# A sixth place for raw weights, spread additions of the seven products, and transposes in a second matrix bank, in a two-layer hybrid decoder on one core

## The chip, the core and the metric

The kernel runs on one core of one Trainium2 chip. Its metric is the device time of one execution in microseconds (us). A core has a matrix engine (TensorE, PE in the profile; its weight loads are shown as PEld), a vector engine (VectorE, DVE), a scalar engine (ScalarE, ACT), GpSimd (POOL) and a queue engine (SyncE, SP) that here issues the loads of weights. Operands lie in an on-chip memory of 128 partitions; products of TensorE are summed in eight banks of a separate memory.

## The reference

256 tokens of width 2048 pass through two layers: differential attention and then a Mamba-2 mixer, each followed by a dense MLP with a squared ReLU, all in float32.

```
for i in range(2):
    hn = rms_norm(h, mixer_norm[i])
    h = h + (diff_attention if i == 0 else mamba2_mixer)(hn, ...)
    h = h + sq_relu_mlp(rms_norm(h, mlp_norm[i]), mlp_w1[i], mlp_w2[i])

sq_relu_mlp(h, w1, w2) = jnp.square(jax.nn.relu(h @ w1)) @ w2    # w1: 2048 x 8192, w2: 8192 x 2048
```

Only the two MLPs matter here. The change also deepens the buffer through which all weights of the kernel pass.

## The kernel before

**How products are kept exact.** Each float32 weight tile of 128x1024 is split into a high part (a cast on ScalarE, L158) and a rest (a subtraction on VectorE, L159); activations are split in the same way (L263, L264, L273, L274). Each product is then three matmuls: high by high, high by rest, rest by high.

**The places.** A raw weight tile is loaded by SyncE into one of five places with the tag `raw` (L183 to L186). Its split goes to one of four places with the tag `w`. The load of a tile waits until the last reader of the earlier tile in its place is done, and SyncE issues its loads strictly one after another. Of the eight banks of TensorE's output memory, three have the tag `aux`, one `aux1`, and four `mm` (the function `bank`, tiles named `pp`).

**The MLP.** The hidden width 8192 is cut into eight blocks of 1024 columns. The first block ("s" in `MLP_KINDS`) is computed plainly by `blocks`: its result is hidden features by tokens, and its activations are split by `expand` straight from `u`. The other seven ("S") are computed by `seven`, a Strassen-like scheme: for each of four slices of the inner width it loads four quarters of the weights, forms sums of them on VectorE (L569, L579, L584, L600, one tile of 128x1024 each), splits them and makes seven products p1 to p7 of a half size, each in a bank of its own. After p1 and p5 come p7, p3 and p6, and last p2 and p4. The sums of products that make the four quarters of the result are formed in `u` on VectorE (L587 to L591, L603, L604), then squared after a ReLU on ScalarE. The result is tokens by features, so `expand` transposes it on TensorE: eight groups of four 128x128 transposes for two blocks (L656), each group in an `aux` bank, from which ScalarE and VectorE split it (L263, L264).

`sum_parts` makes the sums of the activations for the seven products: eight rounds, each with a tile `a` and a tile `asum` from the MLP's own pool (tag `relu`, one place for each).

**The order of the work.** `mlp` first runs blocks 0 and 1 interleaved (`both(0, 28/12)`), with the rounds of `sum_parts` as side work. Then for q = 0 to 3 it multiplies the pair of blocks 2q, 2q+1 by w2 (`token_steps`, L238 and L240, eight steps for each of four column blocks j) while the steps of the next pair's `seven` are interleaved at a fixed rate (`work`, `rate`). `expand` of the pair is put into the side queue at the start of each q. The order in which the instructions stand on each engine is then set by a scheduler in the toolchain, which weighs when places and operands come free; the code's order is only where it starts. So a change of places can move instructions far from the lines that were edited.

In the profile, the first MLP runs from about 404 to 1092 us and the second from about 1765 to 2447 us. The stretch of `both(0)` is 404 to 490 us in the first MLP; the pairs of blocks change over at about 490, 658 and 827 us, and in the second MLP 1358 us later.

Of the kernel before, what the change touches and what calls it, by code (L numbers as in the profile page):

```python
# [20 lines left out]
P = 128  # L21
# [70 lines left out]
def trunk_kernel(ctx: ExitStack, tc: tile.TileContext, x, xt, par, rope, qk, wv, wo, w10, w10s, w20, win, wdt, wout, w11, w11s, w21, out):  # L92
# [25 lines left out]
    def aux():  # L118
        return ps.tile([P, 512], F32, tag="aux", bufs=3, name="aux")
# [60 lines left out]

    def load(src, n=1):

        raw = wp.tile([P, 1024], F32, tag="raw", bufs=5, name="raw")  # L183
        w = 1024 // n
        for i in range(n):
            nc.sync.dma_start(out=raw[:, i * w:(i + 1) * w], in_=src[:, i * w:(i + 1) * w])  # L186
        return raw
# [137 lines left out]
    with tc.tile_pool(name="xin", bufs=1) as xp:  # L325
        raw, xf = [], []
        for s in range(2):
            pool = (wp, xp)[s]
            raw.append([pool.tile([P, 1024], F32, tag="raw", bufs=(5, 4)[s], name="raw") for _ in range(4)])
        for g in range(4):  # L330
            for j in range(2):
                xf.append(xp.tile([P, 2, T], F32, tag="xf", bufs=8, name="xf"))
                nc.sync.dma_start(out=xf[-1], in_=x[2 * g + j])
                if j == 0:
                    for b in range(4):
                        c = slice(512 * (g % 2), 512 * (g % 2 + 1))
                        nc.sync.dma_start(out=raw[g // 2][b][:, c], in_=qk[b, g // 2][:, c])
        w = None
        for g in range(4):
            if g % 2 == 0:  # L340
                w = [wp.tile([P, 2, 1024], F32R, tag="w", bufs=4, name="w") for _ in range(4)]
            for j in range(2):
                xs += x_parts(xf[2 * g + j], 2 * g + j, C_MIX0)
            for b in range(4):
                c = slice(512 * (g % 2), 512 * (g % 2 + 1))
                src = raw[g // 2][b][:, c]
                S.copy(out=w[b][:, 0, c], in_=src)
                V.tensor_tensor(out=w[b][:, 1, c], in0=src, in1=w[b][:, 0, c].bitcast(F32), op=ALU.subtract)
                for i in range(2):
                    for k in range(4):  # L350
                        kk = slice(512 * (g % 2) + k * P, 512 * (g % 2) + (k + 1) * P)
                        act = xs[4 * g + k]
                        if i == 0:
# [171 lines left out]

    def sum_parts(pool, x, dst):

        a = pool.tile([P, 2, T], F32, tag="relu", bufs=2, name="a")
        for i in range(2):
            V.tensor_tensor(out=a[:, i, :], in0=x[i][:, 0, :].bitcast(F32), in1=x[i][:, 1, :].bitcast(F32), op=ALU.add)  # L530
# [12 lines left out]
        s1, s2, s3, s4 = ([sa[:, i, n, :] for i in range(2)] for n in range(4))  # L543
        dst.append([[x0[:, i, 0:P] for i in range(2)], s4, [x1[:, i, 0:P] for i in range(2)], s1, s3, s2, [x1[:, i, P:T] for i in range(2)]])
        yield

    def seven(pool, src, sas, u):
# [42 lines left out]
        V.tensor_tensor(out=u[:, 0, 1], in0=p3, in1=u[:, 0, 1], op=ALU.add)  # L590
        V.tensor_tensor(out=u[:, 1, 1], in0=u[:, 1, 0], in1=u[:, 1, 1], op=ALU.subtract)  # L591
# [12 lines left out]
        V.tensor_tensor(out=u[:, 1, 0], in0=u[:, 1, 0], in1=p4, op=ALU.subtract)  # L604
        for t in range(2):
            S.activation(u[:, t, 0], u[:, t, 0], AF.Relu)
            S.activation(u[:, t, 0], u[:, t, 0], AF.Square)
        yield

    def mlp(xs, w1, w1s, w2, pool, after):  # L610
# [29 lines left out]
        def expand(c, hid, place=None):  # L640
# [8 lines left out]
            for j in range(0, 4, 2):  # L649
                axs = []  # L650
                for i in range(2):
                    ax = aux().rearrange("p (a b) -> p a b", a=2)
                    for f in range(2):
                        for t in range(2):
                            c = T * (j + i) + P * f
                            PE.transpose(ax[:, f, t * P:(t + 1) * P], uf[:, t, c:c + P], ident)  # L656
# [5 lines left out]
        def both(q, share):  # L662

            if not share:
                yield from hidden(2 * q)
# [18 lines left out]
        for _ in both(0, 28 / 12 if kinds[:2] == "sS" else 1.0):  # L684
            pass
        norm_mean()
        V.reciprocal(out=r2, in_=ms)
        for q in range(4):
            if q < 3:
# [387 lines left out]
```

## Time and profile before

| what | us |
|---|---|
| median of three runs (lowest, highest) | 2450.47 (2450.01, 2451.3) |
| profiled execution, its own time | 2449.62 |
| span of the profiled execution | 2447.9 |
| TensorE busy, by the page | 2434.1 |
| VectorE busy | 2098.2 |
| ScalarE busy | 1535.6 |
| share of 16 DMA engines of the queue that loads weights | 61.3% |

The span runs from the first to the last instruction; 1.7 us of the execution's time lie around it. The busy time of TensorE is that of overlapping records: a 128x512 matmul is recorded with 0.39 us, while the next one starts 0.227 us after it, so its modelled end hides the first 0.17 us of a wait. To find lost time on TensorE, the starts of neighbouring rows are to be compared.

### The profile page before, as it was taken

Reading aid. Unit: us, or ns where it says so; the run is one execution under the profiler, and the core shown is the slowest. Engines: PE = TensorE matmul, PEld = TensorE weight load, DVE = VectorE, ACT = ScalarE, POOL = GpSimd, SP = SyncE. Lnnn points to the kernel's source line nnn. Section 1 sums busy time; section 2 is a strip of 40 time slices with the busy share of each in tenths; the row PEclk is TensorE's granted clock in tenths of the full one; section 3 lists DMA queues with packets and bytes.
Section 4 is the critical chain, followed back from the end, with each engine's and each line's share of the span. In section 5 each row is a group of like instructions: output and inputs, shape, how many; then the busy total and the mean of one; then the engine's idle time right before and its main releaser. Section 6 shows DMA issues by size and latency. Waiting matters only on the chain.

```text
span 2447.9 us, 32626 instructions
## 1 busy us (share of the span) xinstructions
PE 2434.1 (99%) x12050; PEld 2038.8 (83%) x12050; DVE 2098.2 (86%) x2591; ACT 1535.6 (63%) x2154; POOL 1.2 (0%) x8
## 2 busy tenths in 40 slices
PE   9999999999999999999999999999999999999999
PEld 8888888878888788888888888888887888878887
DVE  6988879999998999568886887887899999899964
ACT  7666656666666666456776575775666666666653
POOL 0000000000000000000000000000000000000000
PEclk9999999999999999999999999999999999999999
DMA  8545555667667676556565556556566766776764
GB/s 287 164 157 175 167 175 194 208 232 243 230 208 230 221 231 218 191 177 211 190 198 196 174 198 199 166 189 191 190 218 220 239 229 203 238 232 206 233 205 147
DMA packets 140192, 500.54 MB, mean 204 GB/s; under 512 B 15648, under 2 KB 15840, under 8 KB 140032
## 3 DMA queue, kind: packets, MB, share of 16 engines
q1 hardware_dynamic: 137312, 489.75, 61.3%
q10 hardware_dynamic: 2720, 8.71, 1.0%
q8 instruction: 94, 1.54, 0.2%
q14 instruction: 66, 0.54, 0.1%
HBM read 496.24 MB, written 2.16 MB: 204 GB/s over the span
## 4 chain that ended last, share of the span: by engine, by line
PE 70%; DVE 18%; DMA 7%; issue 4%; ACT 1%; DVEq 0%; SPq 0%; ACTq 0%
PE pp L238 21%; PE pp L169 16%; DVE w L159 11%; PE pp L240 10%; PE pp L173 9%; PE aux L557 6%; DMA raw<-in_w11s 3%; DMA raw<-in_w10s 3%; PE aux L559 3%; DVE wsum L569 1%; DVE wsum L600 1%; DVE raw L579 1%; PE aux L878 1%; DVE h L716 1%; ACT w L158 1%
## 5 line engine op out<-in xcount | busy, mean ns | idle before, releaser
L159 DVE TENSOR_TENSOR w<-raw,w 128x1024 fp32r<-128x1024 f32 x858 | 1034.6, 1219 | 196.1 <-ACT w L158 193.5
L158 ACT CAST w<-raw 128x1024 fp32r<-128x1024 f32 x858 | 892.7, 1052 | 493.4 <-PE pp L238 316.3
L238 PE MATMUL pp<-w,act 128*128 128x512 f32 x3072 | 983.1, 391 | 0.7 <-ACT w L158 0.7
L238 PEld LDWEIGHTS pp<-w,act 128*128 128x128 f32 x3072 | 575.4, 188 | 121.7 <-ACT w L158 1.5
L240 PE MATMUL pp<-w,act 128*128 128x512 f32 x1536 | 598.5, 390 | 0.0
L169 PE MATMUL pp<-act,w 128*128 128x512 f32 x2000 | 489.0, 392 | 0.0
L169 PEld LDWEIGHTS pp<-act,w 128*128 128x128 f32 x2000 | 366.4, 188 | 72.6 <-issue 1.0
L240 PEld LDWEIGHTS pp<-w,act 128*128 128x128 f32 x1536 | 288.3, 188 | 58.0
L557 PE MATMUL aux<-w,sa 128*128 128x512 f32 x896 | 300.3, 392 | 5.2 <-DVE act L264 1.7
L173 PEld LDWEIGHTS pp<-act,w 128*128 128x128 f32 x2000 | 258.3, 191 | 11.0 <-issue 0.9
L173 PE MATMUL pp<-act,w 128*128 128x256 f32 x2000 | 266.8, 284 | 0.0
L158 ACT CAST w<-wsum 128x1024 fp32r<-128x1024 f32 x168 | 176.9, 1053 | 114.6 <-PE pp L238 43.8
L557 PE MATMUL aux<-w,act 128*128 128x512 f32 x672 | 228.8, 394 | 0.8 <-ACT w L158 0.3
L159 DVE TENSOR_TENSOR w<-wsum,w 128x1024 fp32r<-128x1024 f32 x168 | 204.8, 1219 | 1.9 <-ACT w L158 1.5
L557 PEld LDWEIGHTS aux<-w,sa 128*128 128x128 f32 x896 | 167.4, 188 | 44.3 <-DVE w L159 4.7
L559 PE MATMUL aux<-w,sa 128*128 128x512 f32 x448 | 175.2, 391 | 0.0
L557 PEld LDWEIGHTS aux<-w,act 128*128 128x128 f32 x672 | 124.8, 188 | 32.2 <-DVE w L159 6.2
L559 PE MATMUL aux<-w,act 128*128 128x512 f32 x336 | 131.4, 391 | 0.0
L559 PEld LDWEIGHTS aux<-w,sa 128*128 128x128 f32 x448 | 84.2, 188 | 16.7
L569 DVE TENSOR_TENSOR wsum<-raw 128x1024 f32<-128x1024 f32 x56 | 68.4, 1222 | 21.4 <-DMA raw<-in_w10s 11.5
L579 DVE TENSOR_TENSOR raw<-raw 128x1024 f32<-128x1024 f32 x56 | 68.5, 1222 | 20.4 <-DMA raw<-in_w11s 11.4
L600 DVE TENSOR_TENSOR wsum<-wsum,raw 128x1024 f32<-128x1024 f32 x56 | 68.0, 1220 | 7.4 <-DMA raw<-in_w11s 3.9
(218 smaller groups left out, 1736.0 us busy)
## 6 DMA issues: line engine op xcount, KB each, us to landing
raw<-in_w SPq DMA_DIRECT2D x288, 512.0 KB, 4.4
raw<-in_win SPq DMA_DIRECT2D x160, 512.0 KB, 4.1
raw<-in_w10s SPq DMA_DIRECT2D x140, 512.0 KB, 4.3
raw<-in_w11s SPq DMA_DIRECT2D x140, 512.0 KB, 4.3
raw<-in_wout SPq DMA_DIRECT2D x64, 512.0 KB, 4.1
raw<-in_qk SPq DMA_DIRECT2D x56, 512.0 KB, 4.3
raw<-in_wv SPq DMA_DIRECT2D x32, 512.0 KB, 4.2
raw<-in_wo SPq DMA_DIRECT2D x32, 512.0 KB, 4.2
```

The lines of the kernel that those rows point to most:

```text
L158: S.copy(out=wh[:, s], in_=raw[:, s])
L159: V.tensor_tensor(out=wl[:, s], in0=raw[:, s], in1=wh[:, s].bitcast(F32), op=ALU.subtract)
L169: PE.matmul(acc, lhsT=wk, rhs=acts[k0 + k], start=(start and k == 0), stop=False)
L173: PE.matmul(acc[:, 0, :], lhsT=wk, rhs=acts[k0 + k][:, 0, :], start=False, stop=(stop and k == 7))
L238: PE.matmul(pp[t], lhsT=act[:, 0, tok], rhs=m, start=(s + i + k == 0), stop=(s == n - 1 and i + k == 2))
L240: PE.matmul(pp[t], lhsT=act[:, 1, tok], rhs=m, start=False, stop=False)
L557: PE.matmul(pp, lhsT=ah, rhs=m, start=(i + kp + j == 0), stop=(i == 3 and kp + j == 2))
L559: PE.matmul(pp, lhsT=al, rhs=m, start=False, stop=False)
L569: V.tensor_tensor(out=a[i], in0=b11, in1=b12, op=ALU.subtract)
L579: V.tensor_tensor(out=b12, in0=b22, in1=b12, op=ALU.subtract)
L600: V.tensor_tensor(out=a[i], in0=a[i], in1=b21, op=ALU.subtract)
L716: V.scalar_tensor_tensor(out=h[:, t, cols(j)], in0=pp[t], scalar=r2[:, t:t + 1], in1=h[:, t, cols(j)], op0=ALU.mult, op1=ALU.add)
```

## The change

1. `raw` has six places and not five. The tiles `a` and `asum` of `sum_parts` are now taken from these six places (each uses half of one), and the tag `relu` is gone.
2. In `seven`, the additions that follow p6 and p7 stay where they were (L587, L588); the three others and their ReLU and square are done one at a time after slices 0, 1 and 2 of p2 and p4 (`u4`, `c12`, `c22`), and the addition of p2 comes with slice 3, ahead of that of p4.
3. The `expand` of block 0 is put into the side queue inside `both`, after the last step of block 0.
4. `expand` puts its second group of each pair of groups in a bank of `mm` (except for blocks 6 and 7, where `place` is set).

```
@@ load, and the first loads of attention
-        raw = wp.tile([P, 1024], F32, tag="raw", bufs=5, name="raw")
+        raw = wp.tile([P, 1024], F32, tag="raw", bufs=6, name="raw")
@@ sum_parts
-        a = pool.tile([P, 2, T], F32, tag="relu", bufs=2, name="a")
+        a = wp.tile([P, 1024], F32, tag="raw", bufs=6, name="a")[:, 0:2 * T].rearrange("p (a b) -> p a b", a=2)
...
-        f = pool.tile([P, 4, P], F32, tag="relu", bufs=2, name="asum")
+        f = wp.tile([P, 1024], F32, tag="raw", bufs=6, name="asum")[:, 0:4 * P].rearrange("p (a b) -> p a b", a=4)
@@ seven
-        V.tensor_tensor(out=u[:, 0, 1], in0=u[:, 0, 1], in1=u[:, 1, 1], op=ALU.subtract)
-        V.tensor_tensor(out=u[:, 0, 1], in0=p3, in1=u[:, 0, 1], op=ALU.add)
-        V.tensor_tensor(out=u[:, 1, 1], in0=u[:, 1, 0], in1=u[:, 1, 1], op=ALU.subtract)
-        for t in range(2):
-            S.activation(u[:, t, 1], u[:, t, 1], AF.Relu)
-            S.activation(u[:, t, 1], u[:, t, 1], AF.Square)
+        def u4():
+            V.tensor_tensor(out=u[:, 0, 1], in0=u[:, 0, 1], in1=u[:, 1, 1], op=ALU.subtract)
+        def c12():
+            V.tensor_tensor(out=u[:, 0, 1], in0=p3, in1=u[:, 0, 1], op=ALU.add)
+            relu2(0, 1)
+        def c22():
+            V.tensor_tensor(out=u[:, 1, 1], in0=u[:, 1, 0], in1=u[:, 1, 1], op=ALU.subtract)
+            relu2(1, 1)
+        late = [u4, c12, c22]
...
             product(p4, A22, split_weights(a[i]), i)
-            yield
-        V.tensor_tensor(out=u[:, 0, 0], in0=p2, in1=u[:, 0, 0], op=ALU.add)
+            if i < 3:
+                late[i]()
+            else:
+                V.tensor_tensor(out=u[:, 0, 0], in0=p2, in1=u[:, 0, 0], op=ALU.add)
+                relu2(0, 0)
+            yield
@@ expand
-                    ax = aux().rearrange("p (a b) -> p a b", a=2)
+                    ax = aux().rearrange("p (a b) -> p a b", a=2) if i == 0 or place is not None else bank()
@@ both
+            side.add(early)
             yield from b
```

How the scheduler's order moves, at three places of the first MLP (the numbers in names count tiles; a lower number was asked for earlier).

VectorE, in `both(0)`. `wsum_3958` is the first weight sum of the seven products and needs the loads `raw_3954` and `raw_3956`; `a_` and `asum_` are tiles of `sum_parts`. Before:

```order
L537 TENSOR_TENSOR asum_3913<-a_3910,asum_3913 128x128
L159 TENSOR_TENSOR w_3852<-raw_3850,w_3852 128x1024
L541 TENSOR_TENSOR sa_3936<-asum_3913,sa_3936 128x512
L319 TENSOR_TENSOR h_101<-pp_3652,h_101 128x512
L319 TENSOR_TENSOR h_101<-pp_3653,h_101 128x512
L159 TENSOR_TENSOR w_3884<-raw_3882,w_3884 128x1024
L530 TENSOR_TENSOR a_3947<-act_3699 128x256 x2
L569 TENSOR_TENSOR wsum_3958<-raw_3954,raw_3956 128x1024
L159 TENSOR_TENSOR w_3921<-raw_3919,w_3921 128x1024
```

and in the changed kernel:

```order
L541 TENSOR_TENSOR sa_3899<-asum_3881,sa_3899 128x512
L535 TENSOR_TENSOR asum_3913<-asum_3913,a_3910 128x128
L159 TENSOR_TENSOR w_3921<-raw_3919,w_3921 128x1024
L274 SCALAR_TENSOR_TENSOR act_3806<-aux_3796,pa_67,act_3806 128x256
L274 SCALAR_TENSOR_TENSOR act_3817<-aux_3801,pa_67,act_3817 128x256
L537 TENSOR_TENSOR asum_3913<-a_3910,asum_3913 128x128
L274 SCALAR_TENSOR_TENSOR act_3806<-aux_3796,pa_67,act_3806 128x256
L274 SCALAR_TENSOR_TENSOR act_3817<-aux_3801,pa_67,act_3817 128x256
L541 TENSOR_TENSOR sa_3936<-asum_3913,sa_3936 128x512
L530 TENSOR_TENSOR a_3947<-act_3699 128x256
L569 TENSOR_TENSOR wsum_3958<-raw_3954,raw_3956 128x1024
```

The weight sum now stands behind the split of `w_3921` and behind a whole round of activation sums. In the built program `raw_3954` has the place that `a_3878` had, and `raw_3956` that of `asum_3881`, whose last reader is the first row here; before, both had places of earlier weight tiles. The loads stand in the same order on SyncE in both kernels.

TensorE, at the change of pairs near 827 us (`w_7181` is the weight sum of p5's first product, `aux_7152` the bank of p5, `w_7225` the first tile of w2 for the new pair). Before:

```order
L656 MATMUL aux_7168<-ident_71,u_5852 128x128 x4
L656 MATMUL aux_7173<-ident_71,u_5852 128x128 x4
L557 MATMUL aux_7151<-w_7198,act_3594 128x512
L559 MATMUL aux_7151<-w_7198,act_3594 128x512
L557 MATMUL aux_7151<-w_7198,act_3603 128x512
L559 MATMUL aux_7151<-w_7198,act_3603 128x512
L557 MATMUL aux_7151<-w_7198,act_3594 128x512
L557 MATMUL aux_7151<-w_7198,act_3603 128x512
L238 MATMUL pp_7221<-w_7225,act_7178 128x512
L238 MATMUL pp_7222<-w_7225,act_7178 128x512
L557 MATMUL aux_7152<-w_7181,sa_3784 128x512
```

and in the changed kernel:

```order
L669 MATMUL aux_7168<-ident_71,u_5852 128x128 x4
L669 MATMUL pp_7173<-ident_71,u_5852 128x128 x4
L557 MATMUL aux_7152<-w_7181,sa_3784 128x512
L559 MATMUL aux_7152<-w_7181,sa_3784 128x512
L557 MATMUL aux_7152<-w_7181,sa_3832 128x512
L559 MATMUL aux_7152<-w_7181,sa_3832 128x512
L557 MATMUL aux_7152<-w_7181,sa_3784 128x512
L557 MATMUL aux_7152<-w_7181,sa_3832 128x512
L557 MATMUL aux_7151<-w_7198,act_3594 128x512
```

The second group of transposes went to a bank of `mm`, and p5 has its `aux` bank at once. The six matmuls of `w_7198` follow, and behind them the next two groups of transposes, one directly after the other.

VectorE, at the additions of the second block of seven products near 630 us (lines L595, L598, L602 of the changed kernel are L589, L590, L591 of before). Before:

```order
L588 TENSOR_TENSOR u_5199<-aux_5389,u_5199 128x512
L159 TENSOR_TENSOR w_5664<-raw_5662,w_5664 128x1024
L589 TENSOR_TENSOR u_5199<-u_5199 128x512
L159 TENSOR_TENSOR w_5681<-raw_5679,w_5681 128x1024
L590 TENSOR_TENSOR u_5199<-aux1_5390,u_5199 128x512
L591 TENSOR_TENSOR u_5199<-u_5199 128x512
L159 TENSOR_TENSOR w_5691<-wsum_5247,w_5691 128x1024
```

and in the changed kernel:

```order
L588 TENSOR_TENSOR u_5199<-aux_5389,u_5199 128x512
L159 TENSOR_TENSOR w_5658<-raw_5656,w_5658 128x1024
L595 TENSOR_TENSOR u_5199<-u_5199 128x512
L159 TENSOR_TENSOR w_5675<-raw_5673,w_5675 128x1024
L159 TENSOR_TENSOR w_5685<-wsum_5247,w_5685 128x1024
L598 TENSOR_TENSOR u_5199<-aux1_5390,u_5199 128x512
L159 TENSOR_TENSOR w_5699<-raw_5697,w_5699 128x1024
```

The split of the weight sum now stands ahead of the last two additions.

More of the change, by code (lines that the diff above doesn't have):

```diff
@@ L328, in trunk_kernel @@
             pool = (wp, xp)[s]
-            raw.append([pool.tile([P, 1024], F32, tag="raw", bufs=(5, 4)[s], name="raw") for _ in range(4)])
+            raw.append([pool.tile([P, 1024], F32, tag="raw", bufs=(6, 4)[s], name="raw") for _ in range(4)])
         for g in range(4):
@@ L588, in seven, with relu2 @@
         V.tensor_tensor(out=u[:, 1, 0], in0=p7, in1=u[:, 0, 1], op=ALU.add)
-        V.tensor_tensor(out=u[:, 0, 1], in0=u[:, 0, 1], in1=u[:, 1, 1], op=ALU.subtract)
-        V.tensor_tensor(out=u[:, 0, 1], in0=p3, in1=u[:, 0, 1], op=ALU.add)
-        V.tensor_tensor(out=u[:, 1, 1], in0=u[:, 1, 0], in1=u[:, 1, 1], op=ALU.subtract)
-        for t in range(2):
-            S.activation(u[:, t, 1], u[:, t, 1], AF.Relu)
-            S.activation(u[:, t, 1], u[:, t, 1], AF.Square)
+        def relu2(t, n):
+            S.activation(u[:, t, n], u[:, t, n], AF.Relu)
+            S.activation(u[:, t, n], u[:, t, n], AF.Square)
+        def u4():
[7 more added lines that the diff above has]
+        late = [u4, c12, c22]
         p2, p4 = aux(), aux()
@@ L601, in seven @@
             product(p4, A22, split_weights(a[i]), i)
+            if i < 3:
[3 more added lines that the diff above has]
+                relu2(0, 0)
             yield
-        V.tensor_tensor(out=u[:, 0, 0], in0=p2, in1=u[:, 0, 0], op=ALU.add)
         V.tensor_tensor(out=u[:, 1, 0], in0=u[:, 1, 0], in1=p4, op=ALU.subtract)
-        for t in range(2):
-            S.activation(u[:, t, 0], u[:, t, 0], AF.Relu)
-            S.activation(u[:, t, 0], u[:, t, 0], AF.Square)
+        relu2(1, 0)
         yield
@@ L660, in expand, with both @@
                     yield
-        def both(q, share):
+        def both(q, share, early=None):
             if not share:
@@ L683, in mlp @@
         side.add(sums_of(), slow=True)
-        for _ in both(0, 28 / 12 if kinds[:2] == "sS" else 1.0):
+        hid = []
+        for _ in both(0, 28 / 12 if kinds[:2] == "sS" else 1.0, expand(0, hid)):
             pass
@@ L688, in mlp @@
         for q in range(4):
-            if q < 3:
+            if q == 0:
+                side.add(expand(1, hid))
+            elif q < 3:
                 hid = []
```

## Prediction

> **What bounds the kernel.** I read the page first, then who waits for whom on TensorE, then the busy times by stage, and at last the rows at the places where TensorE stands still.
>
> ```profile
> span 2447.9 us, 32626 instructions
> PE 2434.1 (99%) x12050; PEld 2038.8 (83%) x12050; DVE 2098.2 (86%) x2591; ACT 1535.6 (63%) x2154; POOL 1.2 (0%) x8
> ```
>
> TensorE is busy 99% of the span, VectorE 86%. The number of matmuls does not change, so the change can only win what TensorE loses in waiting. Its waits, of the whole span:
>
> ```profile
> PE aux L557 <- DVE w L159: 1.8, 3, 1.4
> PE aux L557 <- DVE act L264: 1.7, 2, 1.2
> PE aux L557 <- DVE u L604: 1.5, 2, 0.8
> PE aux L656 <- DVE act L264: 0.9, 2, 0.4
> PE aux L656 <- ACT u L607: 0.7, 2, 0.4
> PE aux L557 <- ACT w L158: 0.3, 2, 0.2
> ```
>
> Columns: us in total, times, longest. All of these lie in the two MLPs, 6.9 us in 13 waits. Each hides 0.17 us more under the modelled end of the matmul before it (0.39 us recorded, next start after 0.227), so about 9 us in all; waits under 0.17 us are not in this list. That is the ceiling for what is easily won: 0.37% of the span. By stage (us, then busy time and count of PE, PEld, DVE, ACT, POOL):
>
> ```profile
> 430.00:460.00 30.00, 29.93 (x148) 24.82 (x148) 29.99 (x34) 19.56 (x24) 0.00 (x0) 1.00 0.68 217
> 460.00:490.00 30.00, 29.43 (x147) 24.69 (x145) 30.00 (x34) 22.68 (x29) 0.00 (x0) 1.00 0.59 197
> 490.00:510.00 20.00, 19.27 (x89) 15.03 (x90) 19.70 (x22) 13.96 (x19) 0.00 (x0) 1.00 0.72 248
> 510.00:655.00 145.00, 144.94 (x638) 119.22 (x637) 137.83 (x131) 91.68 (x99) 0.00 (x0) 1.00 0.69 233
> ```
>
> From 430 to 490 us VectorE is never idle: there it is as much the bound as TensorE. From 510 to 655 it has 7.2 us of slack in 145, and TensorE loses nothing to speak of. The clock is 1.00 throughout.
>
> **Part A, the second bank for transposes, near 827 us.** TensorE:
>
> ```profile
> 826.98 1.04 PE L656 MATMUL aux<-ident,u 128*128 128x128 f32 x8
> 827.77 0.47 PE L557 MATMUL aux<-w,act 128*128 128x512 f32 x1
> 828.09 0.39 PE L559 MATMUL aux<-w,act 128*128 128x512 f32 x1
> 829.24 0.62 PE L238 MATMUL pp<-w,act 128*128 128x512 f32 x2
> 831.05 0.50 PE L557 MATMUL aux<-w,sa 128*128 128x512 f32 x1 [1.19 <-DVE act L264]
> ```
>
> The two L238 end their slots at 829.24 + 2 x 0.227 = 829.69, and p5's first matmul starts at 831.05: 1.36 us lost, because both free `aux` banks hold transposes. In the second MLP the same wait is 1.7 - 1.19 = 0.5 recorded, 0.7 with the hidden part. With p5's bank free, TensorE goes on with 12 matmuls (2.72 us) from 827.77 to 830.5, and only then needs the bank of the first transposes back. VectorE frees it here:
>
> ```profile
> 826.72 1.23 DVE L569 TENSOR_TENSOR wsum<-raw 128x1024 f32<-128x1024 f32 x1 [1.31 <-DMA raw<-in_w10s]
> 827.86 1.41 DVE L716 SCALAR_TENSOR_TENSOR h<-pp,r,h 128x512 f32<-128x512 f32 x2
> 829.18 1.22 DVE L159 TENSOR_TENSOR w<-raw,w 128x1024 fp32r<-128x1024 f32 x1
> 830.32 1.28 DVE L264 TENSOR_TENSOR act<-aux,act 128x512 fp32r<-128x512 f32 x2
> ```
>
> The first of the two L264 ends near 831.0, half a microsecond after TensorE would want the bank. The 1.31 us wait for a load should shrink with a sixth place, but the new order puts another weight sum (1.22 us) ahead of L264, so I leave 831.0. The third pair of groups then waits about as little. Gain 1.36 - 0.5 = 0.85 in the first MLP, 0.3 in the second: **-1.15** (bounds -2.05, both waits gone, and 0).
>
> Where the change of pairs is at 658 us, the same rearrangement meets a dearer order: the sum `wsum_6007` now stands only two splits behind `wsum_5899`, which frees the place of its load.
>
> ```profile
> raw<-in_w10s SPq DMA_DIRECT2D x140, 512.0 KB, 4.3
> ```
> ```profile
> 673.24 0.39 PE L240 MATMUL pp<-w,act 128*128 128x512 f32 x1
> 674.07 0.66 PE L656 MATMUL aux<-ident,u 128*128 128x128 f32 x4 [0.44 <-DVE act L264]
> ```
>
> A load takes 4.3 us from issue to landing and two splits some 2.3 (a 1.22 us row is followed by the next after 1.13, as in 405.31 to 406.44 below), so VectorE would stand 2.0 us. Lost there now: 674.07 - 673.24 - 0.227 = 0.60 and a second wait too short for the list (0.23). Carried through the rows, the L264 that frees the first bank comes 0.7 us after TensorE wants it and a later one 0.3: 1.0 against 0.83, **+0.4** for both MLPs (bounds -1.65, both waits gone, and +2.3, the 2.0 us stall passed on whole in place of 0.83 each).
>
> Groups that now stand in a row save something else. The matmul behind a group takes 828.09 - 827.77 = 0.32 us and not 0.227: each run of transposes costs 0.09. By the order before there are 5, 7 and 7 runs at the three changes of pairs, and 3, 5 and 4 after: 7 fewer, x 0.09 x 2 MLPs = **-1.25** (bounds -1.25 and 0).
>
> **Part B, the spread additions.**
>
> ```profile
> 631.17 0.69 DVE L590 TENSOR_TENSOR u<-aux,u 128x512 f32<-128x512 f32 x1
> 631.78 0.69 DVE L591 TENSOR_TENSOR u<-u 128x512 f32<-128x512 f32 x1
> 632.37 1.22 DVE L159 TENSOR_TENSOR w<-wsum,w 128x1024 fp32r<-128x1024 f32 x1
> ```
> ```profile
> 633.20 0.39 PE L559 MATMUL aux<-w,act 128*128 128x512 f32 x1
> 633.65 0.74 PE L557 MATMUL aux<-w,act 128*128 128x512 f32 x2
> ```
>
> The split at 632.37 stands behind two additions and ends when TensorE already waits: 633.65 - 633.20 - 0.227 = 0.22 us. In the new order the split is ahead of both, 1.2 us earlier. I find such a step at 6 of the 14 places where the additions run, of about this size: 6 x 0.22 = **-1.3** (bounds -3.1, at all 14, and 0). The additions themselves keep their number, and VectorE has slack at all of these places but the first, below.
>
> **Part C, the early expand of block 0**, I cost at nothing. In `both(0)` block 0 gives 12 steps at 28/12, so 28 of the 29 steps of block 1 are out when it ends; the last has no side tick in it, and the queue's order is the same as before. There is no work that must hide anything.
>
> **Part D, the sums in the raw places**, the largest and least certain term. VectorE in `both(0)`:
>
> ```profile
> 405.31 1.22 DVE L159 TENSOR_TENSOR w<-raw,w 128x1024 fp32r<-128x1024 f32 x1
> 406.44 0.76 DVE L530 TENSOR_TENSOR a<-act 128x256 f32<-128x256 f32 x2
> 407.12 1.22 DVE L569 TENSOR_TENSOR wsum<-raw 128x1024 f32<-128x1024 f32 x1
> ...
> 412.39 1.23 DVE L569 TENSOR_TENSOR wsum<-raw 128x1024 f32<-128x1024 f32 x1 [0.51 <-DMA raw<-in_w10s]
> ...
> 420.38 1.23 DVE L569 TENSOR_TENSOR wsum<-raw 128x1024 f32<-128x1024 f32 x1 [0.81 <-DMA raw<-in_w10s]
> ...
> 426.30 1.22 DVE L569 TENSOR_TENSOR wsum<-raw 128x1024 f32<-128x1024 f32 x1 [1.08 <-DMA raw<-in_w10s]
> ```
>
> `a` and `asum` hold two of the six places while the rounds last, so the loads have four, not five. SyncE's order is unchanged, but each load waits longer. By the new order `raw_3956` gets its place when the split sum `sa_3899` is made, about 1.7 us behind the L159 that starts at 405.31 and ends at 406.5: at 408.2. It lands at 408.2 + 4.3 = 412.5, and the first weight sum runs there and not at 407.12, **5.4 us later**. Its two successors get their places from it and its split, and land in turn; other work (the activation rounds) fills most of the gap. Following the new order row by row with these durations, VectorE has done about 2.1 us less by 436 us. As it is never idle from 430 to 490, that lag arrives at the first change of pairs:
>
> ```profile
> 488.82 0.61 PE L557 MATMUL aux<-w,act 128*128 128x512 f32 x2
> 490.19 0.51 PE L557 MATMUL aux<-w,sa 128*128 128x512 f32 x1 [0.76 <-DVE u L604]
> ...
> 491.77 0.33 PE L656 MATMUL aux<-ident,u 128*128 128x128 f32 x1 [0.36 <-ACT u L607]
> ```
> ```profile
> 490.72 1.22 DVE L159 TENSOR_TENSOR w<-wsum,w 128x1024 fp32r<-128x1024 f32 x1
> ```
>
> Lost here before: 490.19 - 488.82 - 0.45 = 0.92 and 0.53 at the transposes, with two short ones 2.06 us. The change removes the first cause: p2's addition (L603) now comes a product earlier, so p5's bank is free. But p5's split, which ended at 490.72 + 1.22 = 491.94, ends at 491.94 + 2.1 = 494.0. Counting 20 matmuls (4.5 us) from p4's last product (ten matmuls ahead of the row at 488.82: 488.82 - 10 x 0.227 = 486.55) to that split's first use, TensorE is there at 491.1 and will have waited 2.9 us in `both(0)` by then; up to the same use it has lost 2.3 now. So +0.6, and 0.15 for the deferred transposes: +0.75 in each MLP, **+1.5** (bounds -4.1, no lag and all of the 2.06 saved, and +10.8, the 5.4 us passed on whole with nothing saved).
>
> The Trainium skill, "DMA: Bandwidth & Descriptors", fits a transfer as about 2.0 us plus its bytes at 436 GB/s (made for GpSimd's queue): an estimate of 3.2 us for 512 KB, by which the lag would be about 1 us less and the whole sum near -3.5. The trace's 4.3 us decides.
>
> **Sum:** -1.15 + 0.4 - 1.25 - 1.3 + 1.5 = -1.8 us. Against the profiled execution, 2449.62, that gives 2447.8; the median of the runs lies 0.85 above it, so I predict **2448.7**.
>
> **Rivals.** *The lag is passed on whole.* If the activation rounds do not fill the gap, the first weight sum's 5.4 us reach TensorE in each MLP: 10.8 in place of 1.5 brings the sum to +7.5, 2458. For it speak the 30.00 of 30 us of VectorE; against it, that TensorE first needs that sum's split ten microseconds later and that 2.4 us of today's waits for loads (0.51, 0.81, 1.08) lie in the same stretch. It decides from a lag of about 4.5 us at 490 us. *No lag.* If VectorE catches up before 490, the 2.06 us go in both MLPs: -4.1 in place of +1.5, sum -7.4, 2443. For it speaks that the lost activation sums are no longer urgent at 436; against it the same two full rows. The Trainium skill, "Perfetto Trace Analysis", Optimization Strategy, says that repeating gaps on the engine that should be full can mean too little room for the next tile; that rule would side with this case, and the waits on L264 and L604 agree with it for `aux`, though no row shows TensorE waiting for a raw place. *The waits only move.* TensorE runs at VectorE's pace at the changes of pairs, and what one wait gives the next takes: 0, 2450.5.
>
> **Chances.** Forecast 0.52 (2446 to 2452), no lag 0.2, whole lag 0.13, moved waits 0.15. 0.2% (4.9 us) is about what a measurement can tell here. Faster than 2445.6: the no-lag case and a tail of the forecast, 0.24; slower than 2455.4: the whole-lag case and a little more, 0.14; between, 0.62. The range that leaves out 2 in 10 reaches halfway into both: 2443.8 to 2455.
>
> **What would show it.** Right: no wait of L557 on L604 or for more than 0.7 us on L264; L569 first at 412 or later; TensorE waits of 2 to 3 us in all between 424 and 440; no steps behind L598 and L602. Wrong: `both(0)` ending more than 3 us later or 1 us earlier than now, a new wait for loads on VectorE between 510 and 655, or matmuls waiting for an `mm` bank.

## The result, and the profile after

The changed kernel takes **2489.05 us** (median of 4 runs, 2483.9 to 2490.54) against 2450.89 for the kernel before on the same chip: ratio 1.0152, interval 1.0135 to 1.017. It is 38 us slower. 2448.7 was forecast, with a range of 2443.8 to 2455.0.

The page of the changed kernel, span and busy times:

```profile
span 2488.6 us, 32595 instructions
PE 2446.1 (98%) x12050; PEld 2043.0 (82%) x12050; DVE 2099.3 (84%) x2591; ACT 1537.9 (62%) x2154; POOL 1.2 (0%) x8
```

No engine has more to do: the matmuls are the same 12050, VectorE's busy time moved by 1.1 us. TensorE's busy time grew by 12 us at the same count, because records overlap less in front of a wait and some matmuls now run slowly (below). The time is lost in waits, and behind some of them in slow matmuls. Who waits for whom on TensorE (us in total, times, longest):

```profile
PE aux L669 <- DVE act L264: 13.4, 5, 3.6
PE aux L557 <- DVE w L159: 13.4, 20, 1.7
PE aux L557 <- ACT w L158: 5.6, 6, 1.5
PE pp L169 <- ACT w L158: 2.8, 2, 1.6
```

(L669 and L733 are L656 and L716 of the kernel before.) The waits on L604 and on the transposes' squares are gone, as the change set out to do; in their place stand larger ones on L264 (the rest of an activation split) and on both halves of the weight splits. What VectorE itself waits for, first before and then after:

```profile
DVE wsum L569 <- DMA raw<-in_w10s: 11.5, 11, 2.9
DVE wsum L569 <- DMA raw<-in_w11s: 9.9, 11, 2.3
```
```profile
DVE wsum L569 <- DMA raw<-in_w10s: 24.5, 15, 3.5
DVE wsum L569 <- DMA raw<-in_w11s: 20.5, 15, 3.4
```

The weight sum L569 stands 45.0 us for its loads and not 21.4, with one place more to load into. By stage (the same first four stretches as in the prediction, and the first change of pairs after 655):

```profile
430.00:460.00 30.00, 26.59 (x127) 20.69 (x126) 26.69 (x28) 19.57 (x24) 0.00 (x0) 1.00 0.76 251
460.00:490.00 30.00, 30.00 (x154) 25.65 (x153) 29.81 (x31) 19.97 (x25) 0.00 (x0) 1.00 0.69 220
490.00:510.00 20.00, 18.43 (x86) 14.08 (x84) 19.59 (x23) 14.39 (x20) 0.00 (x0) 1.00 0.57 187
510.00:655.00 145.00, 144.13 (x632) 118.33 (x633) 134.86 (x127) 91.50 (x97) 0.00 (x0) 1.00 0.72 229
655.00:680.00 25.00, 20.83 (x97) 16.95 (x96) 20.30 (x23) 13.49 (x18) 0.00 (x0) 0.93 0.77 245
```

The last stretch in the kernel before, where its change of pairs lies too:

```profile
655.00:680.00 25.00, 24.50 (x123) 19.70 (x122) 23.44 (x25) 15.90 (x20) 0.00 (x0) 1.00 0.65 219
```

From 430 to 460 TensorE starts 127 matmuls where it started 148, and VectorE, full before, is idle for 3.3 us. From 655 to 680 TensorE starts 97 where it started 123, and its granted clock is 0.93 and not 1.00.

To compare kernels whose stages drift apart, I cut every trace at the same counts of matmuls (those that stand at 404, 490, 640, 690, 810 and 860 us of the kernel before, and in the second MLP at 1765, 1848, 1998, 2048, 2168 and 2218). "Lost" is the sum, over TensorE's rows, of the time from one start to the next above the median of that pair of lines and shape; "stands" is VectorE's idle time that ended with a load into a raw place. The changes of pairs counted apart are those at 658 and 827 us and their like in the second MLP. Both MLPs together, us, one profile each (runs of one kernel differ by 2 to 11 us; a cell shifts by up to 1.5 us with the way in which small differences from the median are counted; the medians come from several chips, on which the kernel before took 2447.9 to 2450.9):

| kernel | median, us | first stretch: lost / stands | four changes of pairs: lost / stands | rest of the MLPs: lost / stands |
|---|---|---|---|---|
| before | 2450.9 | 4.9 / 6.2 | 7.5 / 8.1 | 9.7 / 34.9 |
| changed | 2489.0 | 14.8 / 5.2 | 23.2 / 19.4 | 24.2 / 55.7 |
| e1 places alone | 2488.9 | 16.4 / 4.7 | 27.6 / 26.3 | 17.8 / 47.1 |
| e5 six, own tile | 2481.7 | 4.2 / 2.1 | 27.0 / 25.4 | 22.0 / 47.2 |
| e6 five, lent | 2468.7 | 25.6 / 0.0 | 6.7 / 6.6 | 8.5 / 40.0 |
| e8 five, own tile | 2460.2 | 13.8 / 5.0 | 6.4 / 7.8 | 12.6 / 43.0 |
| e9 six, one given back | 2454.4 | 9.1 / 1.5 | 7.4 / 8.4 | 10.3 / 38.6 |
| e14 changed, one given back | 2462.2 | 22.3 / 4.9 | 4.0 / 8.6 | 10.2 / 38.5 |

Changed against before: 9.9 + 15.7 + 14.5 = 40.1 us lost more, and the spans differ by 40.7. Between the MLPs, in the Mamba-2 mixer, it moved by less than 0.3 us.

**The first stretch.** VectorE's first weight sums, TensorE's waits, and one wait of ScalarE in the changed kernel:

```profile
412.96 1.23 DVE L569 TENSOR_TENSOR wsum<-raw 128x1024 f32<-128x1024 f32 x1 [0.91 <-DMA raw<-in_w10s]
...
433.15 1.22 DVE L569 TENSOR_TENSOR wsum<-raw 128x1024 f32<-128x1024 f32 x1 [1.78 <-DMA raw<-in_w10s]
```
```profile
426.15 0.50 PE L557 MATMUL aux<-w,sa 128*128 128x512 f32 x1 [0.95 <-ACT w L158]
...
435.57 0.73 PE L557 MATMUL aux<-w,sa 128*128 128x512 f32 x2 [0.93 <-DVE w L159]
437.92 1.21 PE L169 MATMUL pp<-act,w 128*128 128x512 f32 x4 [1.62 <-ACT w L158]
```
```profile
436.82 1.04 ACT L158 CAST w<-raw 128x1024 fp32r<-128x1024 f32 x1 [3.44 <-DMA raw<-in_w]
```

The first sum starts at 412.96 in place of 407.12. Places come free in a bunch: six loads are issued between 425.1 and 431.7, the last three of them within 0.9 us, and the last four take 4.5, 5.9, 6.8 and 7.6 us to land. In the kernel before, no load from 404 to 490 us takes over 5.7; in e6 below, which lends places too, three near 434 take 5.7 to 7.4; in e5, which lends none, none takes over 4.7. The last row is ScalarE waiting 3.44 us for one of them; TensorE waits for its result at 437.92.

**A change of pairs.** VectorE in the kernel before, and then in the changed one:

```profile
652.05 1.22 DVE L569 TENSOR_TENSOR wsum<-raw 128x1024 f32<-128x1024 f32 x1 [1.15 <-DMA raw<-in_w10s]
...
656.21 1.41 DVE L716 SCALAR_TENSOR_TENSOR h<-pp,r,h 128x512 f32<-128x512 f32 x2 [0.18 <-PE pp L238]
657.53 1.22 DVE L159 TENSOR_TENSOR w<-raw,w 128x1024 fp32r<-128x1024 f32 x1
658.66 1.22 DVE L569 TENSOR_TENSOR wsum<-raw 128x1024 f32<-128x1024 f32 x1
659.80 1.28 DVE L264 TENSOR_TENSOR act<-aux,act 128x512 fp32r<-128x512 f32 x2
```
```profile
658.77 1.22 DVE L569 TENSOR_TENSOR wsum<-raw 128x1024 f32<-128x1024 f32 x1
659.91 1.22 DVE L159 TENSOR_TENSOR w<-raw,w 128x1024 fp32r<-128x1024 f32 x1
661.04 1.22 DVE L159 TENSOR_TENSOR w<-wsum,w 128x1024 fp32r<-128x1024 f32 x1
665.79 1.23 DVE L569 TENSOR_TENSOR wsum<-raw 128x1024 f32<-128x1024 f32 x1 [3.52 <-DMA raw<-in_w10s]
...
671.65 0.69 DVE L264 TENSOR_TENSOR act<-aux,act 128x512 fp32r<-128x512 f32 x1
```

Before, the second and the third weight sum have the additions into `h` and a split between them, so the third finds its load there, and L264 follows at once. After, the third sum stands ahead of those additions, only two splits behind the second, which frees the place of its load; VectorE stands 3.52 us, and the first L264 starts 12.9 us behind the second sum, where it was 7.8. TensorE meanwhile:

```profile
672.39 1.11 PE L669 MATMUL aux<-ident,u 128*128 128x128 f32 x4 [3.46 <-DVE act L264]
...
674.59 0.63 PE L240 MATMUL pp<-w,act 128*128 128x512 f32 x1
675.01 0.63 PE L238 MATMUL pp<-w,act 128*128 128x512 f32 x1
```
```profile
668.00:672.00 4.00, 0.73 (x2) 0.30 (x2) 4.00 (x6) 1.04 (x1) 0.00 (x0) 1.00 0.90 265
672.00:676.00 4.00, 3.61 (x13) 3.25 (x14) 4.00 (x6) 1.17 (x2) 0.00 (x0) 0.57 0.67 183
```

It waits 3.46 us, and over the next four microseconds its granted clock is 0.57: the matmuls start 0.42 us apart (674.59, 675.01) and not 0.227. About 0.9 us is lost so behind the wait.

### The profile page after: what moved, and what is told of

Its sections match the earlier page's. It is cut to its first block, busy times and chain, and to the rows that moved or that the text cites. A ratio compares the mean times of both kernels' runs of the same rounds, so it can differ in the third digit from the quotient of the medians.

```text
span 2488.6 us, 32595 instructions
## 1 busy us (share of the span) xinstructions
PE 2446.1 (98%) x12050; PEld 2043.0 (82%) x12050; DVE 2099.3 (84%) x2591; ACT 1537.9 (62%) x2154; POOL 1.2 (0%) x8
## 4 chain that ended last, share of the span: by engine, by line
PE 65%; DVE 19%; DMA 9%; issue 4%; ACT 2%; DVEq 0%; SPq 0%; ACTq 0%
PE pp L238 18%; PE pp L169 17%; DVE w L159 11%; PE pp L240 9%; PE pp L173 9%; PE aux L557 5%; DMA raw<-in_w10s 5%; DMA raw<-in_w11s 4%; PE aux L559 2%; ACT w L158 1%; DVE wsum L611 1%; DVE wsum L569 1%; DVE wsum L584 1%; DVE h L733 1%; PE aux L895 1%
## 5 line engine op out<-in xcount | busy, mean ns | idle before, releaser
L557 PEld LDWEIGHTS aux<-w,sa 128*128 128x128 f32 x896 | 165.9, 188 | 62.3 <-DVE w L159 20.7
L569 DVE TENSOR_TENSOR wsum<-raw 128x1024 f32<-128x1024 f32 x56 | 68.4, 1224 | 45.1 <-DMA raw<-in_w10s 24.5
L579 DVE TENSOR_TENSOR raw<-raw 128x1024 f32<-128x1024 f32 x56 | 68.5, 1223 | 25.6 <-DMA raw<-in_w11s 13.4
```

Of the source, the lines that this page charges most:

```text
L557: PE.matmul(pp, lhsT=ah, rhs=m, start=(i + kp + j == 0), stop=(i == 3 and kp + j == 2))
L569: V.tensor_tensor(out=a[i], in0=b11, in1=b12, op=ALU.subtract)
L579: V.tensor_tensor(out=b12, in0=b22, in1=b12, op=ALU.subtract)
```

## The experiments

**e1 to e4: which part.** Each of the first three kernels has one part of the change, the fourth all but the first part.

```
e1: raw bufs 5 -> 6; a, asum from wp tag "raw"
e2: expand: every second group from bank() in place of aux()
e3: u4, c12, c22 after slices 0 to 2 of p2/p4, p2's addition with slice 3
e4: the whole change with raw bufs 5, and a, asum from pool tag "relu"
```

> Only the first part of the change is in this kernel: six raw places, with the activation sums in them. The traces put the lost 40 us into three groups: the stretch with the activation sums (TensorE's excess 0.9 -> 6.8 us in the first MLP, 2.2 -> 7.8 in the second: +11.5), the three changes of pairs of each MLP, where the transposes wait 2.8 to 3.8 us for L264 (about +18 with the slowed matmuls behind), and waits of p1 to p7 on the weight splits in between (about +10). Theory 'places' (the sixth place and the sums in it move VectorE's order and make its loads late everywhere): nearly all of it here, +30 to +40 us, 2480 to 2490. Theory 'two causes' (places cost only the stretch with the sums, the second bank the changes of pairs): +11 to +15, 2462 to 2466. Theory 'together' (only the combination hurts): under +8.

> Only the fourth part: every second group of transposes in a bank of the second matrix; five raw places as before. Theory 'places': no loss, -3 to +2 us against before (my own terms of the forecast, -1.15 + 0.4 - 1.25 = -2). Theory 'two causes': +15 to +22, since all four changes of pairs near 672, 849, 2053 and 2227 us lose 3 to 5.5 us there. Theory 'together': under +8.

> Only the second part: the additions spread over the slices of p2 and p4. My term was -1.3 us, bounds -3.1 and 0, for the u-additions, and a further gain up to -4.1 because the wait of TensorE for L604 at 490 us should be gone without the lag of the sums: -1 to -5. 'Places' and 'two causes' both expect that; a theory that the additions pull ScalarE's casts late (u L591 now waits 26 + 18 us for VectorE where L593 waited 17) expects +3 to +10.

> The whole change without its first part: five raw places, the sums in their own place, everything else as in the changed kernel. 'Places': 2443 to 2450, all of the loss gone. 'Two causes': 2465 to 2475, the changes of pairs still lose. 'Together': 2445 to 2455.

Measured: e1 2488.94 us, ratio 1.0166 (1.0151 to 1.0181); e2 1.0002 (0.9993 to 1.0011); e3 1.0000 (0.9991 to 1.0009); e4 0.9998 (0.9989 to 1.0007). The places alone make the whole loss, the three other parts together nothing that can be measured. "Two causes" and "together" fall: e1 has the old banks and the same waits on L264 at the same places. ScalarE's longer waits on VectorE, which I named as a risk of the spread additions, cost nothing.

**e5, e6, e8: the sixth place or the lent places.** `sum_parts` can work in place in one tile, so that six places and a tile of their own for the sums fit.

```
e5: raw bufs 6; a = pool.tile(tag="relu", bufs=1); a22 = a21 + a22; a21 = a11 - a21; a11 = a22 - a11; a12 = a12 - a11
e6: raw bufs 5; a, asum from wp tag "raw"
e8: as e5, raw bufs 5
```

> Six raw places, but the activation sums not in them: sum_parts works in place in one tile of its own (a22 takes S1, a21 takes S3, a11 takes S2, a12 takes S4), so no raw place is lent out. Everything else as before the change. Theory 'sixth place' (the scheduler uses the extra place to plan VectorE's weight sums closer to their loads, and the loads are later than it plans): the stretch with the sums is free (-11), the changes of pairs and the waits of p1 to p7 stay lost: +22 to +30 us, 2470 to 2480, with waits of 3.6 us on L264 near 848 and 2222. Theory 'lent places' (the sums in the raw places shift the places of all that follow): within 5 us of before, 2444 to 2453.

> Five raw places as before, with the activation sums lent two of them; everything else as before. Theory 'sixth place': only the stretch with the sums pays, and more than with six since three places are left for loads there: +8 to +20 us, all of it in 404 to 500 and 1765 to 1860 us, and no wait over 1.5 us on L264 later. Theory 'lent places': +30 to +50, the changes of pairs lose as in the changed kernel.

> Control for the sums worked in place: five raw places, sums in one tile of their own with half the room. All theories: within 4 us of before; more would mean that the place for a new round's sums (one, not two) delays VectorE in the stretch 404 to 490 us, and that much is to be taken off the run with six places.

Measured: e5 2481.69, a little above the 2480 that I had set as its upper end, ratio 1.0142 (1.0125 to 1.0159); e6 2468.68, 1.0087 (1.0072 to 1.0102); e8 2460.24, 1.0049 (1.0032 to 1.0066). The control e8 is not within the 4 us that I expected: one tile for the rounds in place of two costs 8.9 us in the first stretch (13.8 against 4.9), so e5 has to be read against it. The table then splits cleanly. The sixth place behind the first stretch costs 30 us in each way of having it: e5 less e8 is 20.6 + 9.4, e1 less e6 is 20.9 + 9.3. In the first stretch it gives back 9.6 and 9.2. Lending places there costs 20.7 with five (e6 less before). The changed kernel's first stretch, +9.9, is lending with six.

**e9, e14: the sixth place given back.** A tile that nothing else uses holds one place from the end of the first stretch to the end of the MLP.

```
+ kept = wp.tile([P, 1024], F32, tag="raw", bufs=6); V.tensor_copy(out=kept[:, 0:2], in_=r2)    # after both(0)
+ V.tensor_tensor(out=kept[:, 2:3], in0=kept[:, 0:1], in1=h[:, 0, 0:1], op=ALU.add)             # behind the last q
e9: in e5     e14: in the changed kernel
```

> The kernel with six places and the sums in a tile of their own (+33 us), but one of the six is occupied from the end of the first stretch to the end of the MLP by a tile that nothing else uses (two tiny VectorE instructions per MLP). Theory 'planned order' (with a free place more, the weight sums are planned ahead of L716 and L264 at the changes of pairs, and stand there for a load): the order behind 490 us falls back to that of the kernel before, so all of the loss goes, 2444 to 2453, with no wait over 1.5 us on L264 and VectorE's waits for loads near 50 us. Theory 'first stretch' (the six places of the first stretch leave the loads in a bad phase for what follows): still +15 to +30, 2464 to 2480.

> The changed kernel with all four parts, and one raw place occupied from the end of the first stretch to the end of the MLP. If the loss of the changed kernel is the sum of two terms, the lent places in the first stretch (+10) and the sixth place behind it (+24 to +28), only the first stays: 2456 to 2464, with TensorE's excess of 6 to 8 us in the first stretch of each MLP and the rest as without the first part. If the two depend on each other: over 2468 or under 2453.

Measured: e9 2454.39, ratio 1.0019 (1.001 to 1.0028), 1.4 us above the range that I gave it, and e14 2462.23, 1.006 (1.0045 to 1.0075). Against the kernel before on the same chip, the occupied place takes the loss from 32.8 to 4.1 us in e5's kernel and from 38.2 to 14.3 in the changed one: 29 and 24 us. VectorE's order at the four changes of pairs is in e9 again that of the kernel before, row for row (so it is in e6 and e8), and in e14 that of e4; with six places it is another (in e1, 33 to 36 of the 45 or 46 rows of a change stand in the same order). e5 and then e9 near 655 us:

```profile
648.84 1.23 DVE L569 TENSOR_TENSOR wsum<-raw 128x1024 f32<-128x1024 f32 x1 [2.37 <-DMA raw<-in_w10s]
...
654.58 1.22 DVE L569 TENSOR_TENSOR wsum<-raw 128x1024 f32<-128x1024 f32 x1
...
661.38 1.23 DVE L569 TENSOR_TENSOR wsum<-raw 128x1024 f32<-128x1024 f32 x1 [3.31 <-DMA raw<-in_w10s]
```
```profile
651.67 1.22 DVE L569 TENSOR_TENSOR wsum<-raw 128x1024 f32<-128x1024 f32 x1
...
655.33 1.23 DVE L569 TENSOR_TENSOR wsum<-raw 128x1024 f32<-128x1024 f32 x1 [1.29 <-DMA raw<-in_w10s]
...
661.81 1.22 DVE L569 TENSOR_TENSOR wsum<-raw 128x1024 f32<-128x1024 f32 x1
```

With the sixth place, the first sum is planned earlier, ahead of two additions and three splits that e9 does while the load is under way, and stands 2.37 us; the third is planned early as well and stands 3.31. Together 5.7 us against 1.3. In e14 the loss behind the first stretch is 14.2 us, where the kernel before has 17.2: with five places free the other parts do no harm.

**e10: the sixth place for one load only.** If plain tiles wasted the place, keeping it for the second load of the weight sum should help. The sums have a tile of their own, as in e5.

```
- b11, b12 = load(src[0, i]), load(src[1, i])
+ b11, b12 = load(src[0, i]), load(src[1, i], tag="rawq")     # raw bufs 5, rawq bufs 1
```

> Six places, sums in a tile of their own, but the sixth is for one kind of load alone: the second quarter of p1/p5's weight sum (b12 at L566), which only that sum reads. The plain tiles then have five places as before and can't be fetched earlier than before. 'Planned order' in the form that plain tiles take the sixth place: 2445 to 2456. In the form that any load of a sum that can be planned earlier is planned too early: 2460 to 2480 (the order of VectorE has the sums 5 to 6 rows apart at 490 us and 6, 3, 8 at the next change, between the two kernels).

Measured: 2478.43, ratio 1.0118 (1.0104 to 1.0132); 17.4 us lost and 19.9 stood at the changes of pairs, less than in e5 (27.0 and 25.4) and far more than in e8 (6.4 and 7.8). Who gets the place is the smaller part of it; as I read it, a sum whose load can be asked for earlier is planned earlier, and stands.

**e7, e12: loads asked for earlier.** With five places, the pairs of loads are asked for one slice ahead (e7); e12 adds parts two to four of the change.

```
- b11, b12 = load(src[0, i]), load(src[1, i])
+ b11, b12 = pair                     # pair = the two loads of slice i, asked for after p1's product of slice i - 1; b12, b22 likewise
```

> The kernel before, five places, but each pair of loads for the sums of seven is asked for one slice earlier in the code (L566, L578), ahead of the products of the slice before. If VectorE's waits for loads (49 us in the kernel before, 80 in the changed one) come from the loads of the sums standing behind loads of plain tiles that are not needed for another 4 to 6 us, this takes waits away: VectorE's waits for raw loads 20 to 40 us, TensorE 1 to 6 us faster, 2443 to 2449. If they come from the way VectorE's order is planned, nothing changes: 2446 to 2452 and 45 to 55 us of waits.

> A candidate for a faster kernel: parts two to four of the change (spread additions, early split, second bank) with five places, and the pairs of loads asked for one slice earlier. Parts alone measured 1.000, 1.000 and 0.9998 of before, the earlier loads 1.000. From the waits in the traces (excess of TensorE in the MLPs 22 us before, 20 with the three parts, 21 with the earlier loads) 2443 to 2449 is expected: at best 0.2% faster. If the extra room in VectorE's order is planned away, as with the sixth place, 2455 or more.

Measured: e7 ratio 1.0000 (0.9991 to 1.0009), with 39.5 us of VectorE's waits for loads where there were 48.9: the waits fell as far as I said for the case that gains 1 to 6 us, and the time did not. e12 2446.53 against 2450.26, ratio **0.9985** (0.9976 to 0.9993): beats both kernels, by less than I said could be told from no change. Its trace shows 33.4 us of such waits and 13.2 us lost in the MLPs in place of 22.1.

**e11, e13: taking the sum out of L264's way.** e11 makes the 56 sums on GpSimd; e13 forces the sums behind L264.

```
e11: nc.gpsimd.tensor_tensor(out=a[i], in0=b11, in1=b12, op=ALU.subtract), in e5
e13: V.tensor_copy(out=a[i][:, 0:1], in_=newest[0][:, 1, 0:1]) ahead of the sum, newest[0] = the last tile that L264 wrote, in e5
```

> Six places, sums in a tile of their own, and the 56 weight sums of L569 on GpSimd in place of VectorE, so that a sum that waits for its load no longer holds up the L264 and L159 behind it on VectorE. 'Planned order': the waits of 3.6 to 4.2 us on L264 near 840 and 2213 us go, 2445 to 2465 (GpSimd's own sum is slower, its time unknown here; if it is above 4 us the splits of the sums come late instead and the gain is eaten). If L264 is late for another reason (its ScalarE half, the banks): 2475 to 2485 and the same waits.

> Six places, sums in a tile of their own (+33 us), and each weight sum of p1/p5 may be planned only behind the newest L264: a copy of one column from that L264's result into the sum's tile stands ahead of the sum (22 tiny VectorE instructions per MLP). VectorE's order at the changes of pairs becomes split, L716, L716, split, L264, L264, sum, where it was sum, L716, L716, split, L264, L264. 'Planned order' (the loss is L264 standing behind a sum that waits for its load): the waits of 3.6 to 4.2 us near 840 and 2213 us and of 2.0 near 667 and 2038 are gone and 10 to 20 of the 33 us come back, 2460 to 2472 (some is paid anew, since the sums and their splits now come later). 'Load itself' (the weight sum's own split is what TensorE needs at that place, so it doesn't matter who stands first): no gain, 2478 to 2490, with waits on L159 in place of those on L264.

Measured: e11 2614.49, ratio 1.0667 (1.0644 to 1.0691); e13 2492.12, 1.0179 (1.0164 to 1.0194). Both fail, and both take longer than I had set out for any case. In e11 a sum takes 3.3 us where VectorE takes 1.2, and the waits move to what needs it:

```profile
L569 POOL TENSOR_TENSOR wsum<-raw 128x1024 f32<-128x1024 f32 x56 | 183.8, 3283 | 2226.8 <-PE pp L238 1222.7
```

In e13 TensorE's wait for L264 near 840 us (3.6 in e5) falls to 1.6, and VectorE stands 10.1 us for loads at the changes of pairs in place of 25.4. But TensorE loses about 28 us there, as in e5, two waits of 4.1 us among it: L264 now waits for its ScalarE half, and TensorE for the split of the late sum:

```profile
DVE act L264 <- ACT act L263: 22.9, 20, 1.5
```
```profile
PE aux L559 <- ACT w L158: 19.0, 10, 4.0
```

So "L264 stands behind the sum" is not the whole of it: TensorE needs both at this place, and with the sum put last it is the sum's own split that comes late. Less standing of VectorE is no gain by itself.

**e15: four places.**

```
- raw bufs=5
+ raw bufs=4
```

> The kernel before with four raw places and nothing else changed. It tells whether five is a peak. 'Planned order' does not say by itself; with fewer places every load is asked for later, VectorE's waits for loads should rise as well: 60 to 100 us of them, 2465 to 2500. If fewer places make the scheduler plan the sums later and nothing else, within 5 us of before.

Measured: 2493.5, ratio 1.0182 (1.0165 to 1.0199). Five is a peak: four and six both lose. But four loses elsewhere (8.3 us at the changes of pairs, 48.7 in the rest), on ScalarE's half of the splits, and VectorE's waits for loads rise only to 54 us, less than I expected:

```profile
PE aux L557 <- ACT w L158: 20.1, 27, 3.5
```

## Why the prediction was wrong

**The starting point held.** TensorE is the bound, only its waits in the MLPs can move, and they do; only the ceiling of 9 us was low, since 22.1 us are lost from start to start in the MLPs of the kernel before. The step that failed is what I let the sixth place do behind 490 us. I took it for a cover that shortens waits for loads. I saw in the order that the sum `wsum_6007` stands two splits behind `wsum_5899` and priced that one place at +0.4; near 827 us I counted a gain, and for everything else behind the first stretch I gave the sixth place no price, without a reason. The runs showed +15.7 us at these changes and +14.5 in the rest. Two of the signs that I had named for being wrong came: by the count of matmuls the first stretch ends 4.7 us later, and between 515 and 648 us VectorE stands 3.2 us for the loads of L569, where it stood 0.6.

**Part A, +0.4 at 658 us.** The place was right, the size not. I set the standing at 2.0 us, from a load of 4.3 us; with four loads under way three of them took 5.3 to 5.8, and VectorE stood 3.52. I then carried 1.0 us through to TensorE; it lost 0.87 on a split, 3.6 on L264 and about 0.9 in the slow clock. The bound of +2.3 for both MLPs assumed that the standing would be passed on in place of today's loss and without the clock; the runs showed that here it is passed on whole. At the four changes of pairs, lost and stood are 7.5 and 8.1 before, 23.2 and 19.4 after, 27.6 and 26.3 in e1, 27.0 and 25.4 in e5; e13, with about 28 and 10.1, shows that the two need not go together.

**Part A, -1.15 near 827 us.** I wrote that the 1.31 us wait for a load should shrink with a sixth place. It grew to 2.7, and a weight sum of 1.22 us behind it comes ahead of L264, as the new order said. In place of a gain, one wait of 3.6 us.

**Part A, merged transposes -1.25, and part B, -1.3.** e2, e3 and e4 put their effect within 0.11% of nothing: gains of this size can't be excluded, nor are they shown. In e2's trace the changes of pairs do lose less (3.2 us for 7.5), and the rest loses more (15.0 for 9.7), as the rival that waits only move has it; it is one profile, of the slowest of e2's runs.

**Part C**, at nothing, was not tried by itself; e4 contains it.

**Part D, +1.5.** The mechanism was right as far as it went: lent places make the weight sums late, the first at 412.96, and TensorE waits between 424 and 446. That I had 412.5 is in part luck: the load that ends the wait was issued 0.3 us earlier than I said and took 5.0 us, not 4.3. The term was mis-sized: 5.4 us of waits there and not 2.9, since the loads bunch up, and I gave every load 4.3 us. The longest wait, at 437.92, does not come by VectorE's lag at all but by ScalarE's wait for a late load. And I let the waits in the stretch stand in place of those at 490; they came on top (3.0 us lost from 490 to 510, 2.1 before). Measured, +9.9 for both MLPs: the rival that the lag is passed on whole, at 10.8, comes near in size, though not by its way alone. Its total of 2458 misses too, because the loss behind the stretch, 30 us, stood in none of my cases.

The Trainium skill, "Perfetto Trace Analysis", Optimization Strategy, says that repeating gaps can mean too little room for the next tile. Here one more tile of room cost 20 us net (e1 against e6); by e15 the rule holds from four to five, not from five to six.

**Shown and not shown.** Shown: the sixth place costs about 30 us behind the first stretch, it does so with VectorE's order changed and VectorE standing longer for loads, and giving the place back restores the order and nearly all of the time. Loads that are slower throughout are not the reason: for the two kinds that the sums read, the median is 4.3 us in the kernel before and 4.3 in e5. Not shown: that the order is the cause apart from the late loads, since e13 brought new waits; what time the scheduler reckons for a load; and, row by row, the 9 of the 30 us that lie outside these four changes. All but some 20 of about 560 raw loads in the changed kernel's MLPs were issued within 0.1 us of their place coming free, so for nearly all loads it is the place and the sum's position in the order, not the queue, that set when they are issued.

## What to carry to other kernels

Room for one more tile changes the order that a scheduler makes, and an in-order engine stands wherever its new order puts a load's reader too close behind what frees the load's place. Before adding a place, look in the new order for readers that moved ahead of ready work, and price the standing by the load's time under traffic (here 5.3 to 5.8 us), not by the median (4.3). Where the engine behind it has no slack, as at the changes of pairs here, take all of the standing as lost, and add the matmuls at half pace that can follow. Moving the reader back by hand is no sure cure: in e13 its result came late in turn.

## What the runs showed of the hardware that I had not expected

A wait of TensorE can have a tail. In the changed kernel some 32 matmuls of the MLPs start about 0.2 us late behind long waits, over 6 us of the 40; the kernel before has next to none. The tail does not follow from the length alone (waits here from start to start, with the hidden 0.17 us): behind 3.6 us at 672 they are slow up to 675.8, behind 1.4 us at 1815 eight are (shorter waits stand just ahead), behind 2.0 us at 667 in e5 five (one of 1.7 us stands 3 us ahead), and behind 3.46 us near 510 in e13 none. The Trainium skill, "TensorE: Matmul & The Clock Gate", Part 1, gives half clock after an idle window of about 3.4 us that runs free of the kernel; the row at 672 (clock 0.57, starts 0.42 us apart) agrees with the half, and the missing tail with a window that runs free. The tails behind 1.4 and 2.0 us came without an unbroken idle stretch of 3.4 us; there the measurement decides. No run shows the window itself.

A load of 512 KB has a median of 4.2 to 4.5 us by kind, and the last of six that are issued within 6.7 us took 7.6.
